# A hybrid RG-LRU / gated-DeltaNet trunk on one core: SiLU as one ACT function, an order generator with traced latencies, and small tables in two loads

## The chip, the cores and the metric

The kernel runs on one core of one Trainium2 chip. The core has a matmul engine (TensorE, PE), a vector engine (VectorE, DVE), an activation engine (ScalarE, ACT), a general engine (GpSimd, POOL) and a queue that issues all transfers here (SyncE, SP). The metric is device time in microseconds of one execution; lower is better. Each engine runs its own instructions in program order, and engines wait for each other by semaphores.

## What is computed

Two layers over 2048 frames of width 1024, all in float32. The reference, cut:

```python
c_act = silu(c)
for i in range(2):
    shift, scale, gate = split(c_act @ ada_w[i] + ada_b[i])
    h = rmsnorm(x, norm_g[i]) * (1 + scale) + shift
    out = rglru_block(h) if i == 0 else gated_deltanet_block(h)
    x = x + gate * out
return rmsnorm(x, final_g)

def rglru_block(h):            # layer 1
    xb, zg = split(h @ in_w)   # 1024 x 2048
    xf = causal_conv4(xb) + conv_b
    r, i = sigmoid(per-block 128x128 matmuls of xf + gate_b)
    a = exp(-8 * r * softplus(-lam));  b = sqrt(1 - a*a) * i * xf
    hseq = scan(h_t = a_t h_{t-1} + b_t)
    return (hseq * silu(zg)) @ out_w

def gated_deltanet_block(h):   # layer 2, 8 heads of 128
    proj = h @ in_w            # 1024 x (4096 + 16)
    q, k, v = split(silu(causal_conv4(proj[:, :3072])));  z = proj[:, 3072:4096]
    # l2 norms of q and k, decay g and beta from the last 16 columns,
    # then the chunked delta rule: a triangular solve per chunk and a state recurrence per head
    o = rmsnorm(delta_rule(q, k, v, g, beta)) * onorm_g
    return (o * silu(z)) @ out_w
```

## The kernel before

Matmuls run in a fast fp32 form on split operands: each weight or activation is a high part (`whi`, `hh`) and a low part (`wlo`, `hl`), and each product takes three matmuls of 128x128 by 128x512 (`products`, L668). Layer 1's input projection (tiles `mm`) runs in two halves of 1024 frames, each of two chunks of 512 (`in1`, u = 0 and 1); then comes the out projection (`mmo`); then layer 2's input projection in two halves (`in2`), with the delta rule's small matmuls (`pk`, `pkk`, `pqk`, `px`, `pr`, `pp`, `py`, `pS`) woven between the large ones; then the second out projection with the final norm. Weight panels of 512 KB come through two buffers (tag `raw`), are split by ACT (`whi`, L644) and POOL (`wlo`, L650) in the first half, and reloaded from DRAM in the second.

The order on every engine is written by a generator inside the kernel, class `Weave`. Each piece of work is a Python generator, a thread, that yields what it needs next: an event, a buffer slot, a time on an engine ("dve", 0.6) or a load ("sp", bytes). `Weave.run` keeps a clock for each engine, takes whichever thread could start earliest (a thread's number decides ties), and emits its instruction. Nothing of this clock exists on the chip; it only fixes who stands behind whom. After an instruction the thread's own time is its end plus a pause, `LAG`, 0.2 us after PE and POOL and 0.3 us after ACT and DVE unless the yield names another. ACT's table loads are not in this clock, nor is it known that DVE and POOL can block each other.

The places that the change touches:

- `first_small_thread`, `first_loads_thread`, `columns_thread`: the start. Three small loads (c, a table of biases, the norm gains) stand around the first x loads; then 8 transfers of 512 KB of conditioning weights; then eight more small tables (L374); then two weight panels; then 8 more transfers of conditioning weights. From the sums (`adac`, `adaps`) come shift and scale (`cond`), without which no activation can be split (`split_thread`). `columns_thread` also computes a softplus of 8 columns on DVE (L248 to L260).
- `panels_thread` loads weight panels in the order of use; `out_weights_thread` loads the out projection's weights through the same `raw` buffers (`oraw`, split into `oh` and `ol`, L907 and L909). `xr_thread` loads the rows for the residual.
- `conv2_thread`: a layer-2 chunk. ACT copies the projection out of PSUM (`xe`), POOL makes the first tap (L997), DVE adds three taps (`taps`, L718), then SiLU. The conv weights are halved at the start, so that with x half the conv, SiLU is (1 + tanh x) x: ACT's tanh (L1009) and one DVE operation (L1014) that writes `kt`, `qt` or `vt`. `zgate_thread` does the same for z (L1023, L1025).
- `gates_thread` (layer 1): ACT uses tanh, exp and sqrt, DVE the rest; `pg` are its gate matmuls, which need `xh` (ACT) and `xl` (DVE, L801).
- `key_thread`, `recurrence_thread`: ACT's exp of the decays (`ec`), and the state's chain pp, zt, py, yt, pS, state.

Of the kernel before, what the change touches and what calls it, by code (L numbers as in the profile page):

```python
# [8 lines left out]
F32 = mybir.dt.float32  # L9
# [6 lines left out]
D = 1024  # L16
# [11 lines left out]
POOLED = ""  # L28
# [6 lines left out]
EPS = 1e-6  # L35

# [25 lines left out]
class Thread:  # L62
    def __init__(self, gen, prio, t):
        self.gen, self.prio, self.t, self.want = gen, prio, t, None


class Weave:

    SEEN = 0.92
    LAG = {"pe": 0.2, "act": 0.3, "dve": 0.3, "pool": 0.2}

    def __init__(self):
        self.free = dict.fromkeys(("pe", "act", "dve", "pool", "sp", "dma"), 0.0)
        self.threads = []  # L80
        self.now = 0.0
# [19 lines left out]
    def start(self, th):  # L101
# [8 lines left out]
        return max(th.t, self.free.get(w[0], 0.0))  # L110

    def run(self):
        while self.threads:
# [7 lines left out]
            w, value = th.want, None  # L121
            th.t = t
# [8 lines left out]
            elif w[0] == "none":  # L131
                th.t = t + max(w[1], 0.0)
            else:
                self.free[w[0]] = t + w[1]
                th.t = t + w[1] + (w[2] if len(w) > 2 else self.LAG[w[0]])
# [4 lines left out]
def trunk_kernel(ctx, tc, x, c, ada_w, ada_b, ada_c, norm_c, final_g, w1, cw1, cb1, gate_w, gate_b, lam, ow1,  # L140
                 w2, wab, cw2, a_log, dt_bias, onorm, ow2, out):
# [37 lines left out]

    c_col = cp.tile([P, KT], F32, name="c_col")  # L180
# [17 lines left out]
    tags |= {f"tf{n}": ("l1", 1) for n in range(6)}  # L198
    tags |= {t: ("ps", 2) for t in ("mm", "tp", "c", "d")}
    tags |= {t: ("l1", n) for t, n in {"xh": 2, "xf1": 2, "tg": 4, "th": 2, "tz": 2, "gw": 1, "gh": 1, "gl": 1, "ada": 1, "ng": 1}.items()}  # L200
# [37 lines left out]
    STT, EV, CP, TR, MM, M4 = 0.665, 0.605, 0.48, 0.109, 0.2163, 0.218  # L238
# [24 lines left out]
    def finish_columns(layer, part, d, src):  # L263
# [3 lines left out]
        yield "dve", 0.08, 0.13  # L267
        dve.tensor_tensor(cl, src, ada_s[:, layer, part, sl], ALU.add)
        if part == 1:
            yield "dve", 0.08  # L270
# [10 lines left out]
    def first_loads_thread():  # L281

        yield ev("loaded", (("in1", 0), 0))
        for n, (part, d) in enumerate(FIRST):
            if n == 2:
                yield ev("firstpanels")
            p = hp if n < 2 else pools["hc"]
            raw = p.tile([P, KT, TC], F32, tag=f"h{'hl'[n % 2]}{'BC'[n // 2]}", name=f"ada{n}")
            w.set(ev("adaraw", n), raw)
            for q in range(4):  # L290
                yield "sp", 512 * KB, False
                sp.dma_start(out=raw[:, 2 * q:2 * q + 2, :], in_=ada_w[0, 2 * part + d, :, 2 * q:2 * q + 2, :])
                w.spawn(arrive_thread(ev("adaload", n, q)), 0)
            w.set(ev("adaissue", n))
# [5 lines left out]
    def first_small_thread():  # L300
        for dst, src in ((c_col, c), (ada_s, ada_c), (norm_s, norm_c)):
            yield "sp", 8 * KB, dst is c_col
            sp.dma_start(out=dst, in_=src)
        ttok = yield slots["yf"]
        c_bc = tile_([P, KT, P], "yf", "c_bc")
        yield "act", 0.3
        th = tile_([P, KT], "ss", "c_th")
        act.activation(th, c_col, AF.Tanh, scale=0.5)
        yield "dve", 0.2
        dve.scalar_tensor_tensor(th, th, 1.0, c_col, ALU.add, ALU.mult)  # L310
        dve.tensor_scalar(c_col, th, 0.5, None, ALU.mult)
        w.set(ev("c"))
        yield "dve", 1.57
# [4 lines left out]
    def first_pe_thread():  # L318

        c_bc, ttok = yield ev("cbc")  # L320
        for n in (0, 2):
# [8 lines left out]
            yield "dve", 0.61, 0.13  # L330
# [4 lines left out]
            yield "dve", 0.61, 0.13  # L335
# [6 lines left out]
    def first_dve_thread():  # L342

        yield ev("c")
        for n in (1, 3):
# [3 lines left out]
            for k in range(KT):  # L349
                yield ev("adaload", n, k // 2)  # L350
                yield "dve", STT, 0.13
# [5 lines left out]
            yield "pe", 1.5  # L357
# [1431 lines left out]
```

## Time and profile before

| | |
|---|---|
| timed runs | 1940.69, 1935.67, 1934.42 us (median 1935.67) |
| profiled execution, its span | 1937.1 us, 1.4 over the median |
| PE, DVE, ACT, POOL busy | 1844.0, 1471.2, 1048.2, 654.8 us |
| mean granted PE clock | 0.984 |
| DMA | 322.77 MB, mean 167 GB/s |
| table loads on ACT | 53, of them one in layer 2 |

The profile is of one execution. It gives the busy time of each engine, and for idle time what ended it. PE's busy time is that of pipelined matmuls that overlap (0.39 us each, one begun every 0.23), so busy is not the same as full. A row of a timeline reads: start, length, engine, line, operation, tiles written and read; in brackets the engine's idle time ahead of it and what ended that. A row of waits reads: who, at which line, for whom, us in total, how often, the longest.

### The profile page before, as it was taken

What the parts mean: (1) busy time and instruction counts of PE and PEld (TensorE: products, weight loads), DVE (VectorE), ACT (ScalarE), POOL (GpSimd) and SP (SyncE); (2) the same over time, 40 slices, a digit from 0 to 9 for tenths busy, and PEclk for the clock granted to TensorE, in tenths of its full rate; (3) what the DMA queues carried; (4) which work ended last, traced back from release to release, by engine and by line L of the source; (5) the groups of instructions that cost most, each with busy time, mean ns of one, the idle gap of its engine ahead of it and who ended that gap; (6) DMA issues with size and microseconds to landing.
All of it is one profiled execution on the core that took longest, in us unless ns stands there. A gap on an engine that the chain in (4) does not pass through costs nothing.

```text
span 1937.1 us, 31289 instructions
## 1 busy us (share of the span) xinstructions
PE 1844.0 (95%) x10286; PEld 1503.9 (78%) x10286; DVE 1471.2 (76%) x3175; ACT 1048.2 (54%) x2587; POOL 654.8 (34%) x1116
## 2 busy tenths in 40 slices
PE   6999999999899999898999999999999999999998
PEld 3787778878688877677787877788888888888887
DVE  6898998887544668869888896769777878886653
ACT  3666677667212345375565663565666656654321
POOL 3344542223100235345445543333332334411110
PEclk9999999999899999999999998999999999999999
DMA  8476746554578735446676565555365555687751
GB/s 320 116 219 189 223 138 220 175 167 138 169 204 236 208 106 145 128 111 160 166 186 141 138 158 150 149 156 158 102 163 143 140 140 139 155 246 207 230 161 66
DMA packets 511723, 322.77 MB, mean 167 GB/s; under 512 B 371268, under 2 KB 439236, under 8 KB 511560
## 3 DMA queue, kind: packets, MB, share of 16 engines
q1 hardware_dynamic: 511560, 320.77, 59.1%
q8 instruction: 81, 1.33, 0.3%
q14 instruction: 82, 0.67, 0.1%
HBM read 219.93 MB, written 100.73 MB: 166 GB/s over the span
## 4 chain that ended last, share of the span: by engine, by line
PE 61%; DVE 20%; DMA 6%; issue 4%; ACT 4%; SPq 3%; POOL 2%; DVEq 0%; POOLq 0%; ACTq 0%
PE mm L668 31%; PE mmo L668 16%; DVE xf L718 2%; DVE ttmp L1292 2%; DVE tblk L1295 2%; PE pg L807 1%; PE py L1429 1%; PE pp L1412 1%; PE pS L1442 1%; PE pqk L1257 1%; PE pS L1441 1%; PE pp L1413 1%; PE pkk L1169 1%; DVE xf L756 1%; DMA raw<-in_w 1%
## 5 line engine op out<-in xcount | busy, mean ns | idle before, releaser
L718 DVE SCALAR_TENSOR_TENSOR xf<-xe,cw_s,xf 128x512 f32<-128x512 f32 x288 | 224.9, 784 | 20.6 <-POOL xf L997 18.1
L650 POOL TENSOR_TENSOR wlo<-raw,whi 128x1024 fp32r<-128x1024 f32 x48 | 120.9, 2519 | 143.6 <-ACT whi L644 115.4
L1292 DVE TENSOR_TENSOR ttmp<-blk,tblk 128x60 f32<-128x60 f32 (+24 forms) x496 | 125.4, 253 | 16.6 <-DMA blk<-blk_d 5.4
L1295 DVE TENSOR_TENSOR tblk<-tblk,ttmp 128x60 f32<-128x60 f32 (+24 forms) x496 | 124.8, 252 | 10.7
L644 ACT CAST whi<-raw 128x1024 fp32r<-128x1024 f32 x96 | 100.2, 1044 | 50.3 <-DMA raw<-in_w 44.5
L668 PE MATMUL mmo<-oh,yh 128*128 128x512 f32 x256 | 102.1, 399 | 4.8 <-ACT oh L907 4.8
L668 PE MATMUL mm<-hh_('in2', 0)_5342,whi 128*128 128x512 f32 x256 | 105.3, 411 | 0.0
L668 PE MATMUL mm<-hh_('in2', 0)_5437,whi 128*128 128x512 f32 x256 | 105.3, 411 | 0.0
L668 PE MATMUL mmo<-ol,yh 128*128 128x512 f32 x256 | 102.2, 399 | 3.0 <-DVE ol L909 3.0
L668 PE MATMUL mm<-hh_('in2', 0)_5342,wlo 128*128 128x512 f32 x256 | 104.7, 409 | 0.0
L668 PE MATMUL mm<-hl_('in2', 0)_5343,whi 128*128 128x512 f32 x256 | 104.7, 409 | 0.0
L668 PE MATMUL mm<-hl_('in2', 0)_5438,whi 128*128 128x512 f32 x256 | 104.1, 407 | 0.0
L668 PE MATMUL mm<-hh_('in2', 1)_12030,wlo 128*128 128x512 f32 x256 | 104.1, 407 | 0.0
L668 PE MATMUL mm<-hl_('in2', 1)_12219,whi 128*128 128x512 f32 x256 | 104.0, 406 | 0.0
L668 PE MATMUL mm<-hh_('in2', 0)_5437,wlo 128*128 128x512 f32 x256 | 103.9, 406 | 0.0
L668 PE MATMUL mm<-hh_('in2', 1)_12218,whi 128*128 128x512 f32 x256 | 103.6, 405 | 0.0
L668 PE MATMUL mm<-hh_('in2', 1)_12030,whi 128*128 128x512 f32 x256 | 103.5, 404 | 0.0
L668 PE MATMUL mm<-hl_('in2', 1)_12031,whi 128*128 128x512 f32 x256 | 103.3, 403 | 0.0
L668 PE MATMUL mm<-hh_('in2', 1)_12218,wlo 128*128 128x512 f32 x256 | 103.2, 403 | 0.0
L668 PE MATMUL mmo<-ol,oh 128*128 128x512 f32 (+1 forms) x264 | 103.1, 391 | 0.0
L668 PE MATMUL mmo<-oh,ol 128*128 128x512 f32 (+1 forms) x264 | 103.1, 391 | 0.0
L668 PE MATMUL mmo<-oh,oh 128*128 128x512 f32 (+1 forms) x264 | 103.0, 390 | 0.0
(331 smaller groups left out, 5649.8 us busy)
## 6 DMA issues: line engine op xcount, KB each, us to landing
raw<-in_w SPq DMA_DIRECT2D x96, 512.0 KB, 4.2
araw<-in_ada_w SPq DMA_DIRECT2D x32, 512.0 KB, 4.3
xt<-x_d SPq DMA_DIRECT2D x32, 512.0 KB, 4.9
xt_d<-xb SPq DMA_DIRECT2D x192, 64.0 KB, 2.4
xk<-xt_d SPq DMA_DIRECT2D x24, 512.0 KB, 6.1
xt<-in_x SPq DMA_DIRECT2D x16, 512.0 KB, 4.4
ada<-in_ada_w SPq DMA_DIRECT2D x16, 512.0 KB, 8.5
y_d<-tz SPq DMA_DIRECT2D x32, 256.0 KB, 3.2
```

The lines of the kernel that those rows point to most:

```text
L644: act.copy(hi, raw)
L650: pool.tensor_tensor(lo, raw, f(hi), ALU.subtract)
L668: pe.matmul(pt, lhsT=lhs[a][:, k, :], rhs=rhs[b][:, k, :], start=(k == 0 and n == 0), stop=(k == KT - 1 and n == 2))
L718: dve.scalar_tensor_tensor(xf, xe[:, 1 + j:1 + j + TC], wc[:, j:j + 1], xf, ALU.mult, ALU.add)
L756: dve.scalar_tensor_tensor(xf[:, 3:TC], pt[:, j:j + TC - 3], wc[:, j:j + 1], xf[:, 3:TC], ALU.mult, ALU.add)
L807: pe.matmul(pg, lhsT=a[:, g, :], rhs=b, start=(q == 0), stop=(q == 2))
L1169: pe.matmul(pkk[:, b, :], lhsT=kc, rhs=kc, start=True, stop=True)
L1257: pe.matmul(pqk[:, b, :], lhsT=kt[:, b * P:(b + 1) * P], rhs=qt[:, b * P:(b + 1) * P], start=True, stop=True)
L1292: dve.tensor_tensor(tmp, blk[:, j, j + 1:32].unsqueeze(2).to_broadcast([P, r, c_]), t[:, j, 0:c_].unsqueeze(1).to_broadcast([P, r, c_]), A ...
L1295: dve.tensor_tensor(t[:, j + 1:32, 0:c_], t[:, j + 1:32, 0:c_], tmp, ALU.subtract)
L1412: pe.matmul(pp[:, 0, :], lhsT=kc, rhs=S_, start=True, stop=True)
L1413: pe.matmul(pp[:, 1, :], lhsT=qc, rhs=S_, start=True, stop=True)
```

## The change

Four things are edited together.

1. **SiLU in layer 2 is one ACT instruction.** The tanh and the DVE operation after it are gone in `conv2_thread` and `zgate_thread`, and with them the halving of the conv weights and of the out norm's gain.
2. **The generator's numbers.** Nearly every yield gets another duration. The pauses are 0.2 (PE), 0.128 (ACT), 0.113 (DVE) and 0.034 us (POOL), and most explicit ones go. ACT's yields may name a table set, and a change of set costs 1.28 us in the clock. Kinds "dve2" and "pool2" stand for instructions that use the port shared by DVE and POOL: one that would start inside the other's interval starts at its end. A PE instruction of a thread that did not just run on PE gets 0.12 us for its weights.
3. **Small tables in two loads.** `head` (c, biases, norm gains, lambda, a_log; 36 KB) and `small` (conv weights and biases, gate biases, dt_bias, out norm; 82 KB) stand ahead of x. The softplus no longer waits for the first `cond`.
4. **Waits for panels.** The first weight panel goes ahead of the conditioning weights, the second follows the first 8 transfers of them, and these alternate between the PE and the DVE column block. The first panels of layer 2 wait until all loads of the out projection's weights are issued.

Also, four low halves at the start move from POOL to DVE, four early jobs use other PSUM banks, and a `POOLED` branch in `conv2_thread`, which was off, is gone.

```diff
+LAG = {"pe": 0.2, "act": 0.128, "dve": 0.113, "pool": 0.034}
+WEIGHTS = 0.12
+TABLE = 1.28
+SHARED = {"dve2": "pool2", "pool2": "dve2"}
...
-        return max(th.t, self.free.get(w[0], 0.0))
+        free = self.free.get(w[0].rstrip("2"), 0.0)
+        if w[0] == "pe" and th.last != "pe" and th.t > free - 0.1:
+            return max(free, th.t + WEIGHTS)
+        return max(th.t, free)
+    def engine(self, th, t, kind, dur, lag=None, table=None):
+        e = th.last = kind.rstrip("2")
+        if table is not None and table != self.table:
+            t, self.table = t + TABLE, table
+        if kind in SHARED:
+            for a, b in self.held[SHARED[kind]][-6:]:
+                if a <= t < b:
+                    t = b
+            self.held[kind].append((t, t + dur + (0.08 if e == "dve" else 0.0)))
+        self.free[e] = t + dur
+        th.t = t + dur + (LAG[e] if lag is None else lag)
...
     def taps(xe, xf, wc, j0=1):
-            yield "dve", STT, 0.13 if j < 3 else 0.27
+            yield "dve2", 0.663
...
     def panels_thread():
+                if m == 0 and name == ("in2", 0):
+                    yield ev("owissue", 1, 1)
...
-                    for q in panels[0:2]:
-                        ahead.append((yield from panel_load(name, q)))
+                    yield ev("loaded", (("in1", 0), 0))
+                    ahead.append((yield from panel_load(name, panels[0])))
+                    w.set(ev("firstpanel"))
+                    yield ev("adaissue", 1)
+                    ahead.append((yield from panel_load(name, panels[1])))
...
     def conv2_thread(u, kind, h, i, pt, mtok, bank, rtok):
-        yield "act", 0.53
-        tt = tile_([P, TC], "tt", "tt")
-        act.activation(tt, xf, AF.Tanh)
-        yield "dve", EV
+        yield "act", 0.533, LAG["act"], "silu"
         r = tile_([P, TC], kind + "t", kind + "t")
-        dve.scalar_tensor_tensor(r, tt, 1.0, xf, ALU.add, ALU.mult)
+        act.activation(r, xf, AF.Silu)
...
     def zgate_thread(u, h, i, pt, mtok, bank):
-        act.activation(tz, pt, AF.Tanh, scale=0.5)
-        yield "dve", EV
-        dve.scalar_tensor_tensor(tz, tz, 1.0, pt, ALU.add, ALU.mult)
+        act.activation(tz, pt, AF.Silu)
```

What stands where, at three places. First, SP's queue at the start, before, from the conditioning weights on (`ada_141`, `ada_164`; ahead of them stand c, four x loads and two tables):

```order
L292 DMA ada_141<-in_ada_w 128x1024 x4
L292 DMA ada_164<-in_ada_w 128x1024 x4
L374 DMA cw_s<-in_cw 128x32
L374 DMA cb_s<-in_cb 128x8
L374 DMA gb_s<-in_gate_b 128x16
L374 DMA lam_s<-in_lam 128x8
L374 DMA cw_s<-in_cw 128x96
L374 DMA onorm_s<-in_onorm 128x1
L374 DMA alog_s<-in_a_log 128x8
L374 DMA dtb_s<-in_dt_bias 128x8
L606 DMA raw_204<-in_w 128x1024
L606 DMA raw_206<-in_w 128x1024
```

And now, from the queue's first load:

```order
L328 DMA head_s<-in_head 128x72
L331 DMA small_s<-in_small 128x161
L497 DMA xt<-in_x 128x1024 x4
L627 DMA raw_147<-in_w 128x1024
L316 DMA ada_149<-in_ada_w 128x1024
L316 DMA ada_150<-in_ada_w 128x1024
```

The last two alternate three more times; then follow the second panel and the second 8 transfers. The eight tables between the two halves of the conditioning weights are gone.

On DVE, softplus (`sp`, `sp_d`, `sp_e`) stood behind the first `cond`, with the sum of the second half's weights (`acc<-ada_222`) behind it; its first rows before:

```order
L268 TENSOR_TENSOR cond<-adac,ada_s 128x4
L379 TENSOR_SCALAR cw_s<-cw_s 128x96
L380 TENSOR_SCALAR gb_s<-gb_s 128x16
L381 TENSOR_SCALAR onorm_s<-onorm_s 128x1
L382 TENSOR_SCALAR neg<-lam_s 128x8
L248 TENSOR_SCALAR sp_91<-neg 128x8
```

Now its last rows stand ahead of the scaling of x and of all sums:

```order
L405 TENSOR_SCALAR sp4n<-sp_92 128x8
L406 TENSOR_SCALAR sp_92<-sp_92 128x8
L478 TENSOR_SCALAR xt<-xt,rs 128x1024 x2
L410 TENSOR_SCALAR aexp<-aexp 128x8
L478 TENSOR_SCALAR xt<-xt,rs 128x1024 x2
L384 TENSOR_SCALAR acc<-ada_150,c_col 128x512
```

Second, SP's queue around the second block of out-projection weights (`oraw`), before (`raw16` is a layer-2 panel, `xr` residual rows, `x1_d`, `y_d` and `wlo_d2` stores):

```order
L896 DMA oraw_4161<-in_ow1 128x1024
L606 DMA raw16_4163<-in_w2 128x1024
L658 DMA wlo_d2k0_4140<-wlo_4109 128x1024
L970 DMA xr_4188<-in_x 128x512
L970 DMA xr_4242<-in_x 128x512
L896 DMA oraw_4249<-in_ow1 128x1024
L896 DMA oraw_4254<-in_ow1 128x1024
L959 DMA x1_d_70<-xr_4188 128x512
```

And now:

```order
L924 DMA oraw_3947<-in_ow1 128x1024
L895 DMA gw_3971<-in_gate_w 128x256
L924 DMA oraw_3995<-in_ow1 128x1024
L877 DMA y_d_69<-tz_3874 128x512
L924 DMA oraw_4092<-in_ow1 128x1024
L877 DMA y_d_69<-tz_3958 128x512
L924 DMA oraw_4121<-in_ow1 128x1024
L627 DMA raw8_4149<-in_w2 128x1024
L998 DMA xr_4157<-in_x 128x512
```

All four out-weight loads now stand ahead of the first layer-2 panel and of the residual rows.

Third, ACT in layer 2's first half, at the decays (`ec`) of one key chunk, before:

```order
L1128 ACTIVATE ec<-ec,gc 128x128 x2
L1468 ACTIVATE t_7711<-pp,eg 128x128
L1128 ACTIVATE ec<-ec,gc 128x128
L1435 ACTIVATE yt<-py 128x128
L1128 ACTIVATE ec<-ec,gc 128x128
```

And now, for the same chunk:

```order
L1143 ACT_TABLE_LOAD
L1143 ACTIVATE ec<-ec,gc 128x128
L1040 ACT_TABLE_LOAD
L1040 ACTIVATE tz<-mm 128x512
L1143 ACT_TABLE_LOAD
L1143 ACTIVATE ec<-ec,gc 128x128
L1204 ACTIVATE kd<-kd,ec 128x128
```

A SiLU (`tz`) stands between two exps, with a table load on each side. In the whole program table loads go from 53 to 109: 52 to 36 in layer 1, 1 to 73 in layer 2.

More of the change, by code (lines that the diff above doesn't have):

```diff
@@ L121, in run @@
             w, value = th.want, None
+            if t > th.t and not isinstance(w, tuple):
+                th.last = None
             th.t = t
@@ L178, in trunk_kernel, with part_of @@
     pool.tensor_tensor(fold[:, 0:16], ident[0:32, 0:16], ident[0:32, 16:32], ALU.add)
+    small_s = cp.tile([P, SMALL], F32, name="small_s")
+    def part_of(tile_in, at, *shape):
+        n = 1
+        for s in shape:
+            n *= s
+        ap = tile_in[:, at:at + n]
+        return ap.rearrange("p (a b) -> p a b", b=shape[1]) if len(shape) == 2 else ap
+    cw1_s, cw2_s = part_of(small_s, 0, KT, 4), part_of(small_s, 32, 24, 4)
+    gb_s, cb1_s = part_of(small_s, 128, 2, KT), part_of(small_s, 144, KT)
+    dtb_s, onorm_s = part_of(small_s, 152, NH), part_of(small_s, 160, 1)
     c_col = cp.tile([P, KT], F32, name="c_col")
@@ L281, in first_loads_thread @@
     def first_loads_thread():
-        yield ev("loaded", (("in1", 0), 0))
-        for n, (part, d) in enumerate(FIRST):
-            if n == 2:
-                yield ev("firstpanels")
[L287 to L294, printed above, removed]
+        yield ev("firstpanel")
+        for half in range(2):
+            raws = []
+            for n in (2 * half, 2 * half + 1):
+                p = hp if n < 2 else pools["hc"]
+                raws.append(p.tile([P, KT, TC], F32, tag=f"h{'hl'[n % 2]}{'BC'[half]}", name=f"ada{n}"))
+                w.set(ev("adaraw", n), raws[-1])
+            for q in range(4):
+                for n in (2 * half, 2 * half + 1):
+                    part, d = FIRST[n]
+                    yield "sp", 512 * KB, False
+                    sp.dma_start(out=raws[n % 2][:, 2 * q:2 * q + 2, :], in_=ada_w[0, 2 * part + d, :, 2 * q:2 * q + 2, :])
+                    w.spawn(arrive_thread(ev("adaload", n, q)), 0)
+            w.set(ev("adaissue", 2 * half + 1))
+            if half == 0:
+                yield ev("firstpanels")
     def arrive_thread(event, value=True):
@@ L300, in first_small_thread @@
     def first_small_thread():
-        for dst, src in ((c_col, c), (ada_s, ada_c), (norm_s, norm_c)):
-            yield "sp", 8 * KB, dst is c_col
-            sp.dma_start(out=dst, in_=src)
+        yield "sp", 32 * KB, False
+        sp.dma_start(out=head_s, in_=head)
+        w.spawn(arrive_thread(ev("head")), 0)
+        yield "sp", 80 * KB, False
+        sp.dma_start(out=small_s, in_=small)
+        w.set(ev("small"))
+        w.spawn(arrive_thread(ev("tables")), 0)
+        yield ev("head")
         ttok = yield slots["yf"]
         c_bc = tile_([P, KT, P], "yf", "c_bc")
-        yield "act", 0.3
+        yield "act", 0.01, LAG["act"], "exp"
         th = tile_([P, KT], "ss", "c_th")
-        act.activation(th, c_col, AF.Tanh, scale=0.5)
-        yield "dve", 0.2
-        dve.scalar_tensor_tensor(th, th, 1.0, c_col, ALU.add, ALU.mult)
+        act.activation(th, c_in, AF.Tanh, scale=0.5)
+        yield "dve", 0.101
+        dve.scalar_tensor_tensor(th, th, 1.0, c_in, ALU.add, ALU.mult)
         dve.tensor_scalar(c_col, th, 0.5, None, ALU.mult)
         w.set(ev("c"))
-        yield "dve", 1.57
+        yield "dve", 1.6
         for k in range(KT):
@@ L451, in scale_thread @@
         put("tt", ttok)
-        yield "pool", 0.75, MARGIN / 2 if late else 0.2
+        yield "pool", 1.2, MARGIN / 2 if late else 0.2
         rs = tile_([P, 1], "rs", "rs")
@@ L485, in norm_thread @@
         for k in range(KT):
-            bank = "d" if layer == 0 and k % 2 else "tp"
+            bank = "d" if slot == "A" and k % 2 else "tp"
             ptok = yield slots[bank]
-            yield "pe", 4 * TR
+            yield "pe", 0.436
             pt = ps.tile([P, TC], F32, tag=bank, name="tph")
@@ L681, in job @@
         bank = ("d" if layer == 1 else "c") if kind in "vz" else "mm"
+        if name == ("in1", 0) and n < 4:
+            bank = "mm" if n < 2 else "d"
         mtok = yield slots[bank]
         pt = ps.tile([P, TC], F32, tag=bank, name="mm")
-        yield from products(pt, (hi, lo), h, (lambda k: ev("split", (name, i), k)), 0.2275 if layer == 1 else MM)
+        yield from products(pt, (hi, lo), h, (lambda k: ev("split", (name, i), k)))
         if all(q != p for q, _ in jobs[n + 1:]):
@@ L739, in convolve @@
     def convolve(xf, pt, mtok, wc, bias, edge, key, g, bank):
-        yield "act", 0.66 if bias is not None else 0.57, 0.0
+        yield "act", 0.681
         if bias is None:
@@ L854, in gate_thread @@
         tok = yield slots["tg"]
-        yield "act", 0.6
+        yield "act", 0.593, LAG["act"], "exp"
         tg = tile_([P, TC], "tg", "tg")
```

331 lines of the change are left out of this document (151 added, 180 removed).

## The prediction, made before the changed kernel ran

> **What bounds the kernel now.** I read the page first, then the busy time by stage, then TensorE's (PE's) waits in each stage, then single stretches of the timeline.
>
> ```profile
> span 1937.1 us, 31289 instructions
> PE 1844.0 (95%) x10286; PEld 1503.9 (78%) x10286; DVE 1471.2 (76%) x3175; ACT 1048.2 (54%) x2587; POOL 654.8 (34%) x1116
> PE 61%; DVE 20%; DMA 6%; issue 4%; ACT 4%; SPq 3%; POOL 2%; DVEq 0%; POOLq 0%; ACTq 0%
> ```
>
> PE is busy for 1844.0 of 1937.1 us, so all that an order can win on PE is its 93 us of idle time and what the lower clock after idle time costs. No matmul is removed. Where the 93 us lie, by stage (layer 1, out projection 1, layer 2 first half, second half, end):
>
> ```profile
> 58.00:490.00 432.00, 417.52 (x1802) 334.74 (x1800) 374.40 (x556) 297.27 (x426) 166.93 (x146) 0.99 0.59 179
> 490.00:670.00 180.00, 171.57 (x724) 138.06 (x724) 94.22 (x126) 41.45 (x51) 17.64 (x26) 0.97 0.73 210
> 670.00:1260.00 590.00, 549.33 (x3480) 448.74 (x3479) 470.62 (x1183) 326.81 (x981) 266.93 (x463) 0.98 0.56 144
> 1260.00:1750.00 490.00, 486.96 (x3217) 408.85 (x3216) 386.31 (x1081) 306.23 (x959) 161.69 (x386) 1.00 0.59 156
> 1750.00:1937.00 187.00, 180.18 (x938) 149.15 (x937) 105.58 (x148) 53.82 (x135) 20.37 (x59) 0.99 0.53 160
> ```
>
> The columns are stretch, length, then busy time of PE, its weight loads, DVE, ACT and POOL, granted clock, DMA share, GB/s. PE idles 40.7 us in the first half of layer 2 and 3.0 us in the second half. The first 58 us hold another 20 us (93.1 less 73.4). At clock 0.98 the first half of layer 2 gives away up to 0.02 x 590 = 11.8 us more; the stretch 490 to 670 up to 0.03 x 180 = 5.4 us.
>
> **Head: two small loads instead of eleven, softplus early (term A).** In the first row below DMA moves at its full rate, in the next two it does not. That is where SP's queue issues eight tables before the next weights.
>
> ```profile
> 12.00:16.00 4.00, 4.00 (x9) 1.99 (x8) 0.82 (x3) 0.00 (x0) 0.00 (x0) 1.00 1.03 414
> 16.00:20.00 4.00, 4.00 (x19) 2.36 (x18) 3.57 (x5) 0.00 (x0) 0.00 (x0) 1.00 0.78 265
> 20.00:24.00 4.00, 2.09 (x5) 0.57 (x3) 1.87 (x4) 0.16 (x1) 0.00 (x0) 1.00 0.76 234
> ```
>
> The hole is (414 - 265 + 414 - 234) GB/s x 4 us = 1.3 MB, 3.2 us of DMA time. Behind it is DVE: it runs the 24 small operations of softplus until 39.2 and only then sums the second half of the conditioning weights, and PE waits for the sum:
>
> ```profile
> 39.04 0.17 DVE L385 TENSOR_SCALAR sp<-sp 128x8 f32<-128x8 f32 x1
> 39.12 0.48 DVE L353 TENSOR_SCALAR acc<-ada,c_col 128x512 f32<-128x512 f32 x1
> 39.64 0.75 DVE L355 SCALAR_TENSOR_TENSOR acc<-ada,c_col,acc 128x512 f32<-128x512 f32 x1
> ```
> ```profile
> 46.20 1.18 PE L277 MATMUL adac<-ones,acc 128*128 128x1 f32 x8 [4.22 <-DVE acc L355]
> ```
> ```profile
> 57.74 0.39 PE L668 MATMUL mm<-hh_('in1', 0)_476,whi 128*128 128x512 f32 x1
> ```
>
> The new DVE order has softplus ahead of the first scaling, where DVE waits for x anyway. The sum can then start when the weights land. Until the end of those weights 11.7 MB pass (x 2.1, conditioning 8.4, two panels 1.0, tables 0.1); at the 0.41 MB per us of the full-rate row, starting near 3 us, that is about 31.5 us. I add 1.5 for the last landing, 1.5 for two more summing steps (L355, 0.75 us) and the 1.2 of the matmul: 35.7 against 47.4 now (46.20 and 1.18). What follows up to the start of chunk 1 at 57.74 stays as long as it was. So 11.7 us; the first panel, which now goes ahead of the conditioning weights, is in the 11.7 MB. I take -11. Ends: only the DMA hole, -3; also the slow clock behind the wait, -14. Nothing else waits for the eleven loads that vanish; x is issued after two tables instead of one, below 1 us.
>
> **Out weights ahead of layer 2's first panels (term B).** PE's waits from 488 to 510, and SP's queue just before:
>
> ```profile
> PE mmo L668 <- ACT oh L907: 4.8, 2, 3.6
> PE mmo L668 <- DVE ol L909: 3.0, 2, 2.2
> ```
> ```profile
> 476.20 7.80 SPq L970 DMA_DIRECT2D xr<-in_x  x2
> 484.11 0.84 SPq L896 DMA_DIRECT2D oraw<-in_ow  x2
> ```
>
> The second x row load stood 7.5 us at the head of SP's queue for its buffer, with two out-weight loads behind it; a layer-2 panel had taken the raw buffer before them. The added wait holds layer-2 panels until all four out-weight loads are issued; behind it stand only those panels, which PE needs at 670. In the new order all four stand ahead of the panel and of both row loads, so this queueing is gone. 7.8 us of waits plus up to 5.4 of clock: I take -10; ends -13 and 0 (ACT's table loads ahead of these splits could hold them as well).
>
> **Layer 1's order (term C).** PE's largest wait between 50 and 488 is for the low half that DVE computes:
>
> ```profile
> PE pg L807 <- DVE xl L801: 6.8, 7, 1.9
> PE adapt L277 <- DVE acc L410: 2.5, 1, 2.5
> ```
>
> All waits of that stretch add up to 14.3 us. The generator now knows that a DVE operation stands still while POOL holds the shared port, as at 797.53, where the same operation took 1.10 us beside a POOL copy and 0.75 at 798.95:
>
> ```profile
> 797.53 1.10 DVE L718 SCALAR_TENSOR_TENSOR xf<-xe,cw_s,xf 128x512 f32<-128x512 f32 x1
> 798.55 0.21 DVE L1292 TENSOR_TENSOR ttmp<-blk,tblk 128x68 f32<-128x68 f32 x1
> 798.80 0.23 DVE L1295 TENSOR_TENSOR tblk<-tblk,ttmp 128x68 f32<-128x68 f32 x1
> 798.95 0.75 DVE L718 SCALAR_TENSOR_TENSOR xf<-xe,cw_s,xf 128x512 f32<-128x512 f32 x1
> ```
>
> No DVE work leaves layer 1, and DVE is 374 of 432 us busy there, so I take less than half of 14.3: -6. Ends: -14, or +5 if orders that are tighter miss as often in new places.
>
> **Layer 2, first half: SiLU on ACT (term D).** PE waits there almost only for DVE:
>
> ```profile
> PE pk L1135 <- DVE kt L1014: 7.6, 4, 3.9
> PE pp L1412 <- DVE state L1454: 6.4, 7, 1.8
> PE py L1429 <- DVE zt L1421: 5.3, 4, 1.9
> PE pqk L1257 <- DVE qt L1014: 3.3, 1, 3.3
> PE px L1334 <- DVE tf L1327: 3.3, 5, 1.6
> ...
> PE pS L1441 <- ACT yt L1435: 1.8, 2, 1.5
> ```
>
> L1014 and L1025 are the DVE halves of SiLU that go. Their busy time in the same two halves of layer 2:
>
> ```profile
> 670.00:1260.00 590.00, 40.83 (x50) 0.98 0.56 144
> 1260.00:1750.00 490.00, 31.63 (x46) 1.00 0.59 156
> ```
> ```profile
> 670.00:1260.00 590.00, 10.91 (x16) 0.98 0.56 144
> 1260.00:1750.00 490.00, 10.93 (x16) 1.00 0.59 156
> ```
>
> So 51.7 us leave DVE's 470.6 in the first half, 11%, and each k, q and v loses one hop. The ACT instruction stays and changes its function; I give SiLU the time of the tanh in its place. The waits for kt and qt (10.9 of the 40 us) lose their releaser, of the other DVE waits (25 us) I let half go, and half of the 11.8 us of slow clock with them: 9 + 13 + 6 = -28. Ends: -52, all of it, and +10, no gain and a few tighter places.
>
> **Table loads (term E).** Layer 2 had one table load; its new order has 73, half of them in each half, since exp and SiLU alternate; layer 1 falls from 52 to 36. ACT pays per load what the trace shows:
>
> ```profile
> 487.66 0.82 ACT L819 ACTIVATE tg<-tg,sp4n 128x512 f32<-128x512 f32 x1
> 488.49 1.28 ACT L830 ACT_TABLE_LOAD   x1
> 489.79 0.63 ACT L830 ACTIVATE tg<-tg 128x512 f32<-128x512 f32 x1
> ```
>
> The load starts 0.01 us after the operation before it and ends 0.02 before the next, so 1.3 us each, 47 us per half: ACT goes from 327 to 374 of 590 and from 306 to 353 of 490. That lies beside PE's matmuls unless PE's next small matmul waits for the ACT copy behind a load (yt cost PE 1.8 us in the first half). I take +6; ends 0 and +24, half of 37 loads' 1.3 us becoming a PE wait.
> [...]
>
> **Sum.** -11 - 10 - 6 - 28 + 6 = -49 us on the profiled span of 1937.1: 1888. The timed runs' median is 1935.67, 1.4 below that span, so I say 1887 (-2.5%). A change under 0.3%, 6 us, could not be told from none.
>
> **Rivals.**
> 1. Slower: the new order has no slack. The generator's pause after an ACT or DVE result falls from 0.3 us to 0.128 and 0.113, about 0.18. Layer 2 has 544 groups of small matmuls that follow such a result (128 each of pp, py, pS, the rest per key and head). If half of them come 0.18 us too early, PE waits 49 us more; with A and B kept and C and D lost, 1937 - 21 + 49 = 1965. It decides from about 120 such misses if D fails. For it: PE waits only 3.0 us in the second half, under the old pauses. Against: the matmul of the fill work, 0.23 us, is still put between.
> 2. Layer 2 does not move: DVE was late there because of what feeds it. A, B and half of C remain, E too: 1937 - 11 - 10 - 3 + 6 = 1919. For it: the second half has no waits with DVE equally loaded (386 of 490, 79%, against 80%), so load alone is not the cause. Against: 10.9 us of the waits name the removed line.
> 3. ACT becomes the pace: every second load of 73 stops PE for 1.3 us and nothing is won in layer 2: 1937 - 27 + 47 = 1957. Against: 1.8 us of waits for yt.
> [...]
> 4. The head does not do what it says: DMA bandwidth sets it and only the hole goes. A is -3 and the rest as forecast: 1896.
>
> **Chances.** Forecast 0.56, own range 1862 to 1912; rival 2 0.24; rival 4 0.07; rival 1 0.08; rival 3 0.05. Range 1855 to 1930: below, all terms near their good ends at once (-82); above, rival 2 with E at its bad end. Faster 0.86 (forecast, rivals 2 and 4 with a little lost), within 0.3% 0.04, slower 0.10.
>
> **What would show it.** A: the first chunk-1 matmul near 46 and no 4 us wait for adac. B: no waits for oh and ol between the last layer-1 panel and the out projection. C: pg waits for xl under 4 us. D: PE idle in the first half of layer 2 down from 40 to under 20 us and a clock of 0.99 there. E: waits for yt, t2 or kt on ACT of a few us. The prediction is wrong if PE's small matmuls show hundreds of short waits in layer 2, or if waits for ACT take the place of those for DVE.

## The result and the profile after

The changed kernel takes 1954.38 us (median of 4 runs, 1949.76 to 1960.42) against 1935.36 for the kernel before: ratio 1.0091, 95% interval 1.0067 to 1.0114. It is 0.9% slower. The prediction was 1887, 2.5% faster. The profiled execution took 1960.42 us, with a span of 1958.7.

The page of the changed kernel, its first lines and the shares of the chain that ended last:

```profile
span 1958.7 us, 31162 instructions
...
PE 1855.2 (95%) x10286; PEld 1507.1 (77%) x10286; DVE 1382.8 (71%) x3049; ACT 1117.7 (57%) x2643; POOL 618.5 (32%) x1112
...
PE 53%; DVE 15%; DMA 13%; ACT 6%; issue 6%; SPq 4%; POOL 2%; DVEq 0%; POOLq 0%; ACTq 0%
```

The work moved as the diff says: DVE 88 us less, ACT 69 us more (73 table loads in layer 2 among it), the same 10,286 matmuls. Yet PE idles for 103.5 us (1958.7 - 1855.2) instead of 93.1, and it is busy for 11 us longer with the same matmuls. That is the granted clock, 0.979 over the span against 0.984. Busy time by stage, in the columns of the prediction's table:

```profile
58.00:490.00 432.00, 406.27 (x1748) 327.06 (x1747) 354.63 (x532) 275.33 (x407) 150.92 (x144) 0.99 0.57 173
490.00:670.00 180.00, 170.45 (x710) 135.19 (x709) 98.43 (x134) 35.52 (x45) 20.61 (x29) 0.97 0.77 221
670.00:1260.00 590.00, 557.59 (x3488) 455.58 (x3487) 421.32 (x1101) 372.32 (x1016) 248.89 (x461) 0.96 0.55 143
1260.00:1750.00 490.00, 479.41 (x3169) 398.63 (x3168) 347.64 (x1034) 344.88 (x992) 160.42 (x390) 0.99 0.56 143
1750.00:1958.00 208.00, 199.73 (x1013) 163.78 (x1011) 117.12 (x154) 62.41 (x141) 21.11 (x58) 0.99 0.56 179
```

The idle time of layer 2's first half fell from 40.7 to 32.4 us (the forecast was under 20), but its clock fell too, from 0.98 to 0.96, and the second half idles 10.6 us where it idled 3.0. These stretches are cut at fixed times, and layer 2 begins 7.7 us later now. Cut at its own matmuls (the first, the first of the second half, the last large one; the same two lines of the kernel before stand under "Neighbours of the kernel before"):

```profile
676.00:1211.00 535.00, 507.21 (x3161) 417.37 (x3160) 382.64 (x1001) 343.48 (x946) 232.43 (x440) 0.97 0.57 147
1211.00:1765.00 554.00, 536.85 (x3596) 441.83 (x3595) 388.47 (x1140) 377.61 (x1071) 175.72 (x413) 0.98 0.55 146
```

Idle time goes from 38.8 to 27.8 us in the first half and from 4.8 to 17.2 in the second: what the one gives, the other takes. PE's waits in the first half of layer 2:

```profile
PE pr L1361 <- ACT tz L1040: 6.3, 2, 5.3
PE py L1444 <- DVE zt L1436: 4.5, 7, 1.7
PE pp L1427 <- DVE state L1469: 3.4, 7, 0.7
PE pk L1150 <- ACT kt L1032: 3.3, 3, 2.0
```

The waits for DVE's kt and qt are gone; a shorter one for ACT's kt and a new one for tz stand in their place. Over the whole span the accounting is simple: PE's busy time less (1 - clock) x span is 1813.0 us before and 1814.1 after, so the span is that constant, plus idle time, plus what the slow clock takes. Idle time grew by 10.4 us and the slow clock by 10.1 (31.0 to 41.1); together 20.5 of the 21.6 us between the two spans.

For the experiments I cut each span at four places of its trace: the first matmul of chunk 1, the first and the last matmul of layer 1's out projection, and the last of layer 2's. Before: 57.7, 418.3, 191.8 and 1262.3 us between them; after: 54.3, 422.3, 198.9 and 1276.1. With these cuts the two losses lie in different places. Idle time grows in layer 1's panels, from 14.5 to 24.7 us, and hardly in layer 2 with the second out projection, from 43.7 to 44.9. The slow clock takes 5.1 us of layer 1's panels in both kernels, but 27.3 us of layer 2 instead of 13.7: half clock for 54.6 us there instead of 27.3.

### The profile page after: what moved, and what is told of

The parts are those of the page before. It is cut to its first block, busy times and chain, and to the rows that moved or that the text cites. A ratio compares the mean times of both kernels' runs of the same rounds, so it can differ in the third digit from the quotient of the medians.

```text
span 1958.7 us, 31162 instructions
## 1 busy us (share of the span) xinstructions
PE 1855.2 (95%) x10286; PEld 1507.1 (77%) x10286; DVE 1382.8 (71%) x3049; ACT 1117.7 (57%) x2643; POOL 618.5 (32%) x1112
## 4 chain that ended last, share of the span: by engine, by line
PE 53%; DVE 15%; DMA 13%; ACT 6%; issue 6%; SPq 4%; POOL 2%; DVEq 0%; POOLq 0%; ACTq 0%
PE mm L694 28%; PE mmo L694 11%; DMA raw<-in_w 2%; DMA araw<-in_ada_w 2%; DMA blk<-blk_d 2%; PE py L1444 2%; DVE tblk L1310 2%; DVE ttmp L1307 2%; PE pp L1427 1%; DMA x_d<-xr 1%; PE pS L1456 1%; PE pS L1457 1%; PE pp L1428 1%; DVE xf L784 1%; DVE xf L746 1%
## 5 line engine op out<-in xcount | busy, mean ns | idle before, releaser
L746 DVE SCALAR_TENSOR_TENSOR xf<-xe,small_s,xf 128x512 f32<-128x512 f32 x288 | 222.0, 774 | 41.5 <-POOL xf L1025 31.1
L694 PE MATMUL mm<-hh_('in2', 1)_12106,wlo 128*128 128x512 f32 x256 | 105.7, 413 | 0.0
L694 PE MATMUL mm<-hh_('in2', 1)_12106,whi 128*128 128x512 f32 x256 | 105.2, 411 | 0.3 <-DVE tf L1354 0.3
L694 PE MATMUL mm<-hh_('in2', 0)_5431,whi 128*128 128x512 f32 x256 | 104.8, 409 | 0.7 <-ACT tz L1040 0.7
L694 PE MATMUL mm<-hl_('in2', 0)_5432,whi 128*128 128x512 f32 x256 | 105.2, 411 | 0.0
L694 PE MATMUL mm<-hh_('in2', 0)_5302,whi 128*128 128x512 f32 x256 | 105.1, 410 | 0.0
L694 PE MATMUL mm<-hl_('in2', 1)_12107,whi 128*128 128x512 f32 x256 | 104.9, 410 | 0.0
L694 PE MATMUL mm<-hh_('in2', 0)_5302,wlo 128*128 128x512 f32 x256 | 104.2, 407 | 0.0
L694 PE MATMUL mm<-hh_('in2', 1)_11783,whi 128*128 128x512 f32 x256 | 104.0, 406 | 0.0
L694 PE MATMUL mm<-hh_('in2', 1)_11783,wlo 128*128 128x512 f32 x256 | 103.9, 406 | 0.0
```

Source lines behind the costliest of these rows:

```text
L694: pe.matmul(pt, lhsT=lhs[a][:, k, :], rhs=rhs[b][:, k, :], start=(k == 0 and n == 0), stop=(k == KT - 1 and n == 2))
L746: dve.scalar_tensor_tensor(xf, xe[:, 1 + j:1 + j + TC], wc[:, j:j + 1], xf, ALU.mult, ALU.add)
```

## Experiments

Theories: *numbers*, the generator's new figures make worse orders; *tables*, ACT with its table loads is late; *draw*, the order that the generator writes for the kernel before is better than its near neighbours, so whatever changes the order loses that first. In the first four runs *draw* still meant that any order lands within some 10 us of any other; 1987.54 and 2012.89 us ruled that out, and the meaning given here came with the neighbours. Ratios are to the kernel before, with 95% intervals; stages are those above.

### SiLU alone, and everything but SiLU

```diff
 # before_silu: kernel before, k, q, v (z alike); generator numbers old
-        act.activation(tt, xf, AF.Tanh)
...
-        dve.scalar_tensor_tensor(r, tt, 1.0, xf, ALU.add, ALU.mult)
+        act.activation(r, xf, AF.Silu)
 # after_tanh: the reverse, in the changed kernel
```

before_silu: 

> The kernel before (1935) with only layer 2's SiLU moved to ACT's function; the generator keeps its old numbers and does not know of the table loads. Theory numbers (the new figures and pauses of the generator cost the time, SiLU is worth what the prediction gave it): 1935 - 28 = about 1907. Theory tables (ACT, with a load between every exp and SiLU, is what is late in the changed kernel): no gain, 1940 to 1960, with more loads than the 73 of the changed kernel and waits of PE for kt, qt and tz on ACT. Theory draw (each new order lands within some 10 us of any other): 1925 to 1945 without a pattern.

after_tanh: 

> The changed kernel (1954) with the old SiLU: tanh on ACT, product on DVE, all new figures kept. Theory tables: the layer-2 loads go and with them the loss, 1925 to 1938. Theory numbers: it stays slow or gets worse, since DVE is loaded as before and the orders are as tight, 1955 to 1975. Theory draw: 1940 to 1960.

before_silu took 1946.55 us (1.0063, 1.0043 to 1.0082), after_tanh 1987.54 (1.0273, 1.0250 to 1.0297). Taking SiLU back out makes the changed kernel 33 us slower, all of it in layer 2 (1310.8 against 1276.1). That is above all three forecasts, and *tables* wanted 1938 at most. With the old numbers SiLU alone gains nothing: it missed the 1907 of *numbers* by 40 us and lies in the range of *tables*. So these two runs disagree on *tables*; the loads are taken out by themselves further down.

### The numbers alone, and everything but the numbers

```diff
 # after_old_numbers: changed kernel (before_new_numbers: the reverse, in the kernel before)
-LAG = {"pe": 0.2, "act": 0.128, "dve": 0.113, "pool": 0.034}
-WEIGHTS = 0.12
-TABLE = 1.28
-SHARED = {"dve2": "pool2", "pool2": "dve2"}
+LAG = {"pe": 0.2, "act": 0.3, "dve": 0.3, "pool": 0.2}   # no weight pause, table price or port
...
-        yield "dve2", 0.599
+        yield "dve", 0.69, 0.13                          # and all other durations
```

after_old_numbers: 

> The changed kernel with the generator's old durations and pauses, no shared port, no weight pause and no price for a table load; the head, the waits on panels and SiLU on ACT stay. Theory numbers: the loss goes and the gains show, 1885 to 1910. Theory tables: 1950 or more, since the loads are no longer planned. Theory draw: 1930 to 1955.

before_new_numbers: 

> The kernel before with only the generator's new durations, pauses, port, weight pause and table price; head, panels and the tanh form of SiLU as before. Theory numbers: slower, 1950 to 1970, with the short PE waits in layer 2 that the changed kernel has. Theory tables: 1925 to 1938. Theory draw: 1925 to 1950.

after_old_numbers took 1934.35 us (0.9991, 0.9974 to 1.0008), before_new_numbers 2012.89 (1.0407, 1.0390 to 1.0423). The numbers alone cost the kernel before 78 us, the changed kernel only 20. For *numbers* that is the right sign, but its forecast of 1885 to 1910 for the changed kernel without them was missed, and 2012.89 lies above all three forecasts.

### One class of numbers at a time, and the head alone

```diff
 # before_pauses               # before_durations            # before_port
-yield "dve", STT, 0.13        -yield "dve", 0.69, 0.13      -yield "dve", 0.69, 0.13
+yield "dve", STT              +yield "dve", 0.599, 0.13     +yield "dve2", 0.69, 0.13
 # with the new LAG             # with the old LAG            # old LAG, new SHARED
 # head_only: after_old_numbers with the tanh and DVE form of SiLU
```

before_pauses: 

> The kernel before (1935) with one class of the new numbers alone: the generator's pauses after a result (ACT 0.128, DVE 0.113, GpSimd 0.034 us in place of 0.3, 0.3, 0.2, and of the pauses given line by line). All new numbers together made 2013. Theory pauses (results are expected too early, so small matmuls wait): most of the 78 us, 1980 to 2010. Theory durations: 1930 to 1945. Theory port: 1930 to 1945.

before_durations: 

> The kernel before with the new durations alone, old pauses, no port, no weight pause. Theory durations (the traced latencies, most of them longer on PE, shift which work stands where): 1970 to 2010. Theory pauses: 1930 to 1945. Theory port: 1930 to 1945.

before_port: 

> The kernel before with the shared port of DVE and GpSimd alone in the generator, old durations and pauses. Theory port (the model holds work back that the chip would have begun, so what follows is placed late): 1965 to 2000. Theory pauses or theory durations: 1925 to 1945.

head_only: 

> The kernel before with only the tables' two loads, the early softplus, the order of the first panels, the new banks of the first four jobs and the wait of layer 2's panels for the out weights; old numbers, tanh form of SiLU. From the three runs so far (changed kernel with old numbers 1934, before with SiLU alone 1947): 1935 - 12 = 1922 if the parts add. The prediction's terms A and B give 1935 - 21 = 1914. Theory draw: 1925 to 1945.

before_pauses took 1991.78 us (1.0300, 1.0275 to 1.0326), before_durations 1992.10 (1.0290, 1.0261 to 1.0318), before_port 2002.75 (1.0355, 1.0334 to 1.0377), head_only 1940.69 (1.0037, 1.0019 to 1.0056). Each class was to stay near 1935 under the two theories that name another class. Each alone cost 57 to 68 us, and all three together 78: that is no sum of three faults. In head_only the head and the out projection gained 4.6 and 12.6 us, and layer 2, whose instructions it leaves as they are (for the generator z's tanh is 0.017 us longer, and v asks for its buffer earlier), took 1284.2 us instead of 1262.3. Both point to *draw*. A rival is left for the three classes: put among old numbers, a class can count a delay twice (before_port adds port waits to a duration of 0.69 us where the new numbers have 0.599). The neighbours below have no such mixture.

### Neighbours of the kernel before

```diff
 # draw_copy, draw_matmul (kernel before)
-STT, EV, CP, TR, MM, M4 = 0.665, 0.605, 0.48, 0.109, 0.2163, 0.218
+STT, EV, CP, TR, MM, M4 = 0.665, 0.605, 0.49, 0.109, 0.2163, 0.218   # draw_copy
+STT, EV, CP, TR, MM, M4 = 0.665, 0.605, 0.48, 0.109, 0.2170, 0.218   # draw_matmul
 # draw_seen (kernel before), after_draw_seen (changed kernel)
-    SEEN = 0.92
+    SEEN = 0.95
```

draw_copy: 

> The kernel before with one number of the generator changed that says nothing new: the duration of an ACT copy 0.49 instead of 0.48 us (0.48 to 0.52 in the trace). Theory draw (the old numbers were settled on one good order, and any other order costs tens of microseconds whatever the reason for it): 1950 to 1995, like the pauses, the durations and the port each alone. Theory numbers (the three new classes are wrong in themselves): within 6 us of 1934.

draw_matmul: 

> The kernel before with the duration of a large matmul in the generator 0.2170 instead of 0.2163 us, 0.3%. Theory draw: 1950 to 1995. Theory numbers: within 6 us of 1934.

draw_seen: 

> The kernel before with the generator's delay from a transfer's end to its semaphore 0.95 instead of 0.92 us. Theory draw: 1950 to 1995. Theory numbers: within 6 us of 1934.

after_draw_seen: 

> The changed kernel with the same delay 0.95 instead of 0.92 us. Theory draw: the changed kernel was not tuned around its order, so this lands on either side of 1954, 1940 to 1970. Theory numbers: within 6 us of 1954.

draw_copy took 1956.10 us (1.0106, 1.0077 to 1.0134), draw_matmul 1971.24 (1.0197, 1.0174 to 1.0220), draw_seen 1958.94 (1.0138, 1.0103 to 1.0174), after_draw_seen 1947.63 (1.0060, 1.0040 to 1.0080). A duration that is 0.3% longer for the generator, with nothing else changed, costs 36 us; the changed kernel moves by 7 us the other way. The three neighbours of the kernel before came out as *draw* had it. The fourth fits *draw* and lies only 0.4 us outside the range of *numbers* (within 6 us of 1954), so it decides little. The same three edits made to after_old_numbers, in the next section, move it by +5, +10 and -4 us: they do not cost 20 to 36 us in themselves.

Where does such an order lose? Layer 2 in two pieces, cut at the first matmul of its second half, first of the kernel before, then of draw_matmul:

```profile
667.00:1217.00 550.00, 511.24 (x3196) 419.41 (x3195) 442.49 (x1111) 304.57 (x921) 251.88 (x440) 0.98 0.57 144
1217.00:1735.00 518.00, 513.19 (x3434) 428.24 (x3433) 403.60 (x1131) 320.92 (x998) 174.68 (x407) 1.00 0.58 150
```
```profile
667.00:1231.00 564.00, 516.24 (x3118) 422.45 (x3118) 430.62 (x1067) 302.78 (x911) 247.26 (x442) 0.95 0.55 140
1231.00:1766.00 535.00, 527.31 (x3523) 440.49 (x3522) 416.59 (x1188) 326.81 (x1019) 181.15 (x410) 0.99 0.56 147
```

Idle time is 43.6 us before and 55.5 in draw_matmul; the clock falls from 0.98 to 0.95 and from 1.00 to 0.99, which is about 22 us more (0.03 x 564 + 0.01 x 535). No single wait explains it: PE's waits for the state's chain (`state`, `zt`) go from 12 to 27 and from 12.1 to 22.1 us, those for `kt` fall.

### Neighbours of the changed kernel with old numbers, and old pauses

```diff
 # old_numbers_copy, old_numbers_matmul, old_numbers_seen:
 # after_old_numbers with the edits of draw_copy, draw_matmul and draw_seen
 # after_old_pauses: changed kernel
-LAG = {"pe": 0.2, "act": 0.128, "dve": 0.113, "pool": 0.034}
+LAG = {"pe": 0.2, "act": 0.3, "dve": 0.3, "pool": 0.2}   # and the pauses given line by line
```

old_numbers_copy: 

> The changed kernel with old numbers (1934) and the ACT copy at 0.49 instead of 0.48 us in the generator. Theory draw alone (head and SiLU are worth some 25 us, the new numbers nothing; 1934 was a good draw): the three draws of this form average 1940 to 1955, like the changed kernel. Theory numbers and draw (the new numbers cost some 15 us beyond a draw): they average 1930 to 1940, and the out projection of layer 1 takes about 180 us in each.

old_numbers_matmul: 

> As old_numbers_copy, with the large matmul at 0.2170 instead of 0.2163 us. Draw alone: 1940 to 1955 on average over the three. Numbers and draw: 1930 to 1940.

old_numbers_seen: 

> As old_numbers_copy, with the delay from a transfer's end to its semaphore 0.95 instead of 0.92 us. Draw alone: 1940 to 1955 on average over the three. Numbers and draw: 1930 to 1940.

after_old_pauses: 

> The changed kernel with only the pauses set back (0.3, 0.3, 0.2 us and those given line by line); new durations, port, weight pause and table price stay. If the pauses are what the new numbers cost: 1930 to 1940, with layer 1's out projection back at about 180 us. If it is the durations or the port: 1945 to 1960 and an out projection of 190 us or more.

old_numbers_copy took 1939.39 us (1.0021, 0.9999 to 1.0044), old_numbers_matmul 1944.82 (1.0037, 1.0015 to 1.0060), old_numbers_seen 1930.23 (0.9971, 0.9945 to 0.9997), after_old_pauses 1955.47 (1.0091, 1.0062 to 1.0120). The first three average 1938, inside the range of *numbers and draw*; old pauses alone give nothing back in the whole. With all draws of each form:

| head and SiLU | numbers | times, us | mean |
|---|---|---|---|
| old | old, three neighbours | 1956, 1971, 1959 | 1962 |
| new | old, given and three neighbours | 1934, 1939, 1945, 1930 | 1937 |
| new | new, given and one neighbour | 1954, 1948 | 1951 |
| old | old, the kernel before itself | 1935 | |

So the change as a structure (head, panels, SiLU on ACT) is worth about 25 us between such neighbours, the new numbers cost about 14 of it again, and the kernel before stands 27 us below its own neighbours: 1935 + 27 - 25 + 14 = 1951. How the kernel before came by its good order no run shows. Of the 25, about 14 stand in the head (57.7 to 59.2 us with the old structure, 52.7 to 53.3 with the new) and in layer 1's out projection (188.9 to 193.7 against 179.6 to 184.6), where the two groups do not overlap; in layer 1's panels and in layer 2 they do. The 14 us of the numbers are the weakest, from six kernels with 5 to 10 us between neighbours.

The 14 us do show in one stage. Layer 1's out projection takes 179.6 to 184.6 us in the four kernels of the second row, 198.9 and 195.5 in those of the third. Slices of it, first of after_old_numbers, then of the changed kernel:

```profile
500.00:530.00 30.00, 30.00 (x132) 24.38 (x131) 10.67 (x14) 2.92 (x3) 2.37 (x2) 1.00 0.57 188
530.00:560.00 30.00, 30.00 (x133) 24.56 (x132) 16.10 (x22) 4.74 (x8) 2.44 (x6) 1.00 0.74 197
...
620.00:650.00 30.00, 30.00 (x132) 24.53 (x132) 17.55 (x27) 9.35 (x11) 3.90 (x3) 1.00 0.82 245
```
```profile
500.00:530.00 30.00, 30.00 (x132) 24.52 (x131) 17.65 (x25) 3.16 (x3) 2.88 (x4) 1.00 0.71 226
530.00:560.00 30.00, 26.68 (x107) 20.71 (x106) 14.67 (x20) 5.45 (x7) 1.50 (x4) 0.94 0.72 201
...
620.00:650.00 30.00, 28.63 (x123) 22.46 (x122) 14.29 (x19) 5.34 (x7) 1.49 (x4) 1.00 0.81 214
```

With old numbers PE does not stop in these slices; over the whole stage it idles 0.9 us, against 10.7 in the changed kernel and 10.4 in after_draw_seen. The gap at 530 in the changed kernel is a matmul of layer 2's conditioning rows that stands in the midst of PE's out products and needs a sum whose weights are still on their way; PE's row, then DVE's:

```profile
536.32 2.08 PE L442 MATMUL adapt<-acc,ones 128*128 128x512 f32 x2 [3.32 <-DVE acc L431]
```
```profile
532.11 1.22 DVE L957 TENSOR_TENSOR yl<-yf,yh 128x1024 fp32r<-128x1024 f32 x1 [1.67 <-ACT yh L953]
534.73 1.54 DVE L431 SCALAR_TENSOR_TENSOR acc<-araw,c_col,acc 128x512 f32<-128x512 f32 x2 [1.40 <-DMA araw<-in_ada_w]
```

after_old_pauses brings this stage to 187.2 us, so in that order the old pauses give back some 10 of the 15.

### The table loads by themselves, and old durations

```diff
 # after_no_loads: changed kernel, both places in layer 2
-        act.activation(r, xf, AF.Silu)
+        act.activation(r, xf, AF.Tanh)
 # after_old_durations: changed kernel
-        yield "dve2", 0.599
+        yield "dve2", 0.69                               # and all other durations
```

after_no_loads: 

> The changed kernel (1954) with ACT's tanh in place of its SiLU in layer 2, and nothing put in for the missing product, so that layer 2's values differ from the reference's; every instruction stands where it stood, less 72 table loads. Prediction (term E, +6, ends 0 and +24): 1948, between 1930 and 1954. Rival 3 of the prediction (ACT is the pace): 1907. If loads lie beside PE's work altogether: within 3 us of 1954.

after_old_durations: 

> The changed kernel with the old durations alone; new pauses, port, weight pause and table price stay. If the new durations cost the 14 us in layer 1's out projection: that stage back at 180 to 185 us and 1935 to 1945 in all. If it is pauses and port, or no single class: a stage of 190 us or more and 1945 to 1965.

after_no_loads took 1957.19 us (1.0117, 1.0092 to 1.0141) against the changed kernel's 1.0091 (1.0067 to 1.0114): no gain at all. This is the one pair in which no other instruction moves. Layer 2 by itself takes 2.5 us less, with 44.4 us of idle time instead of 44.9 and the same 27.3 us of slow clock. Its page shows ACT busy for 93 us less:

```profile
PE 1856.6 (95%) x10286; PEld 1510.6 (77%) x10286; DVE 1381.3 (71%) x3049; ACT 1024.7 (52%) x2571; POOL 621.5 (32%) x1112
```

PE's largest wait for ACT over the whole span stays without the loads (8.0 us in three waits in the changed kernel):

```profile
PE pr L1361 <- ACT tz L1040: 8.3, 3, 4.5
```

The wait for tz is one of place: in the changed kernel pr stands right behind a large matmul at 992.67 and needs the buffer that ACT's tz empties, and tz stands in ACT's queue behind 6.7 us of scalings and sums of squares that run without a load from 990.85 on; PE's row, then the end of ACT's run:

```profile
998.37 0.25 PE L1361 MATMUL pr<-ac,tf 32*32 32x32 f32 x1 [5.31 <-ACT tz L1040]
```
```profile
996.56 1.04 ACT L471 ACTIVATE sqj<-xt 128x1024 bf16<-128x1024 f32 x1
997.51 0.19 ACT L471 ACTIVATION_READ_ACCUMULATOR sqj<-xt 128x1 f32 x1
997.72 0.60 ACT L1040 ACTIVATE tz<-mm 128x512 f32<-128x512 f32 x1
998.34 1.28 ACT L1143 ACT_TABLE_LOAD   x1
```

after_old_durations took 2065.12 us (1.0669, 1.0642 to 1.0695), the slowest of all: layer 1's panels alone take 499.3 us instead of 422.3. New pauses over old durations are worse than either pure set. One old duration misfits plainly: the 3.1 us of ACT's square root, 0.54 in the new numbers, seems to hold two table loads (0.54 + 2 x 1.28; in the trace of the changed kernel the square root takes 0.63 us and a load ahead of it 1.28), and this run adds the table price on top. Its out projection takes 200.5 us, so the old durations do not give the 14 us back. How the 14 us divide over the classes stays open: each class alone, put in or taken out, makes a new order whose own scatter and misfit are larger than what is sought.

## Why the prediction was wrong, step by step

**The sum.** The step that failed is the one that added terms to "the profiled span of 1937.1". It took the old order as the neutral ground on which parts are set off. A change that reaches the generator replaces the whole order, and three near neighbours of the old one cost 20 to 36 us with no cause but a number changed by 0.3 to 3%. This term, about +27, was in no part of the sum. Of the 67 us between 1887 and 1954 it makes about 27. The structure is worth about 25 instead of the 43 of A, B, D and E, which makes 18, and the new numbers cost about 14 where C took a gain of 6, which makes 20. Rival 1 (1965, chance 0.08) had the sign but not the mechanism: idle time grew in layer 1's panels and not, over all, in layer 2, and layer 2 lost by the slow clock. The range's end of 1930 was also too low for what it was said to hold: rival 2 with E at its bad end is 1937 - 11 - 10 - 3 + 24 = 1937.

**A, head, -11.** Right in sign, less than half in size. Chunk 1 begins 3.4 us earlier here and 4.4 to 5.0 in the five kernels with the new head and old numbers, near rival 4's -3. The last conditioning sum is gone as a wait:

```profile
40.94 0.95 PE L299 MATMUL adac<-ones,acc 128*128 128x1 f32 x8
```

It runs at 40.94, 5.3 us earlier, not 11.7. The forecast of the landing was about right: weights in by 31.5 + 1.5 = 33 us (the 1.5 was the author's estimate, from no row), and the x load that the queue issues next, at 23.33, lands 10.4 us later, at 33.8. What failed is the step from there to the sum. DVE takes three summing steps in a row and then stands still, because the last one is behind a product with PE's own column block:

```profile
33.69 2.32 DVE L386 SCALAR_TENSOR_TENSOR acc<-ada,c_col,acc 128x512 f32<-128x512 f32 x3
39.30 0.69 DVE L363 TENSOR_TENSOR atmp<-adaps,ident 128x512 f32<-128x512 f32 x1 [3.29 <-PE adaps L359]
39.91 0.74 DVE L386 SCALAR_TENSOR_TENSOR acc<-ada,c_col,acc 128x512 f32<-128x512 f32 x1
```

PE runs the last matmuls of that block at 37.38, among chunk 0's matmuls and without a pause before them. From the sum's matmul to chunk 1 it is then 13.3 us, where the sum of the prediction kept the old 11.5. PE itself has no idle time from 27.6 to 49.8. So the landing of these weights no longer sets this stretch, the order on DVE and PE does: 3.4 us is near rival 4's -3, but its reason, DMA bandwidth, is not what these rows show.

**B, out weights ahead of panels, -10.** Right as a mechanism: no wait for oh or ol is left, and with old numbers the out projection takes 182 us on average instead of 191.8. In the changed kernel the new waits shown above took it back (10.7 us of idle time, 8.4 before), and ten matmuls that stood in other stages before, four for conditioning rows and six of the gates, now stand in this one, which makes it longer still; the sum had no term for that stage's other waits.

**C, layer 1's order, -6.** Wrong in sign in this order, within its ends: the panels' stage is 4 us longer, and waits for xl stay at 6.9 us (the forecast was under 4). The neighbour after_draw_seen takes 418.6 us there, like the kernel before, so the sign is that of one order. What the term started from does show in the trace of the kernel before: the 149 taps of L718 with no POOL instruction beside them took 0.70 to 0.76 us, and all 19 that took over 0.78 ran beside one, the longest (2.88 us from 892.83) beside POOL's `wlo`, which ended at 895.17. Beside the row at 797.53 it is the first tap (L997, 1.26 us from 796.83), not a copy. That it is a port that holds DVE up no run shows.

```profile
PE mm L694 <- DVE xf L784: 7.4, 2, 4.1
PE pg L835 <- DVE xl L829: 6.9, 6, 3.2
PE mm L694 <- ACT whi L670: 5.5, 2, 4.7
```

The first and the third are new: a panel's matmul waits for the buffer that the convolution frees, and for the halves of its weights.

**D, SiLU on ACT, -28.** It depends on what it is compared with. Against the same numbers with tanh, layer 2 gains 34.7 us (1310.8 to 1276.1). Against old numbers, five tanh orders average 1278 (1262 to 1296) and five SiLU orders 1273 (1265 to 1283), a gain that their scatter covers. Against the kernel before it is a loss of 14, since that order is the best of the five.

**E, table loads, +6.** Zero within 0.35%, at its lower end. The 1.3 us a load from the trace were right, and of the 93 us in layer 2 at most 2.5 showed there; the rest lay beside PE. Rival 3 is out: 72 loads less, no time less.

**The bound.** That idle PE time is all that there is to win was right; that the slow clock can double while the idle time stays, as in layer 2, was not in the sum (it took half of the 11.8 us of slow clock as won).

## What to carry to other kernels

Where a generator writes the order, one kernel is one draw: before crediting or blaming an edit, shift an irrelevant number by a per cent three or four times on both sides and compare the means. An edit that keeps the order and takes one cost out (here 72 table loads) settles in one run what exchanged numbers cannot. Predict against the mean of the neighbours, not against a kernel that stands below them; old_numbers_seen (1930.23) is below both kernels, but as the best of four draws it says little more.

## What the runs showed of the hardware

The granted clock in the records has two values, 1.00 and 0.50, in pieces of whole multiples of 3.413 us (26 pieces in the kernel before, 34 in the changed kernel; but for the last, which outlasts the program), and at 959.5 us of the changed kernel it drops with no long wait ahead. There, between two stretches of large matmuls, the recurrence runs alone:

```profile
952.00:956.00 4.00, 4.00 (x32) 3.17 (x29) 3.80 (x9) 1.74 (x3) 3.80 (x5) 1.00 0.38 66
956.00:960.00 4.00, 2.51 (x13) 1.62 (x11) 2.42 (x8) 2.02 (x9) 1.71 (x4) 0.94 0.32 131
960.00:964.00 4.00, 2.67 (x9) 1.79 (x9) 3.12 (x11) 1.52 (x8) 1.46 (x3) 0.50 0.15 25
964.00:968.00 4.00, 2.97 (x10) 2.08 (x10) 3.55 (x10) 1.14 (x4) 0.00 (x0) 0.50 0.63 108
968.00:972.00 4.00, 3.78 (x12) 3.30 (x13) 3.58 (x12) 2.18 (x6) 0.00 (x0) 0.50 0.08 15
```

The longest wait from 955 to 972 is 1.0 us, PE is busy for 2.5 of 4 us, and the clock goes to 0.50 at 959.5, for four pieces, 13.7 us. In the trace of the kernel before, cut into 3.413 us windows, 11 of the 12 drops before the last piece follow a window in which PE was busy for at most 0.48 of the time, and one follows a share of 0.63; in the changed kernel 15 of 16 follow a share of 0.63 or less, the one at 959.5 a share of 0.56. Not every such window is followed by a drop: one of 0.46, at 287.1 us in the changed kernel, is not. The half clock lasts 38.6 us in all in old_numbers_seen, 62.7 in the kernel before, 83.0 in the changed kernel and 113.7 in draw_matmul. So a window about half busy was enough for a drop in these two traces, and an order paid twice for a stretch in which only dependent small matmuls were left: from 956 to 972 in the changed kernel 4.1 us of idle time, and 6.2 us more (0.39 x 16) by a granted clock of 0.61.
